# The first two filler weights go through value buffers instead of the stream's raw buffers

## The chip, the cores and the metric

The kernel runs on one core of a Trainium2 chip. The metric is device time in microseconds (us) of one execution, the median of several. A core has a matrix engine (PE), a vector engine (DVE), a scalar engine (ACT), a general engine (POOL) and a sync engine (SP) that here only issues DMAs. Each works through its own instructions in the order in which the program lists them; they wait for each other by semaphores. An instruction that waits holds up everything listed behind it on its engine.

## The reference

One layer over 1024 latent tokens of width 1024 with 256 context tokens. A modulated RMS norm is projected by one wide matrix `w_in` into the inputs of two branches, a gated linear attention (GLA) and a differential attention, and into two merge gates:

```
pl = project(modulate(x, sh_x, sc_x), w_in[layer])
o_gla = bidir_gla(q, k, v, la_f, la_b, s_f, s_b)
a = softmax(s1) - lam * softmax(s2);  o = a @ v          # per head, per block of queries
...
y = sigmoid(m_gla) * (a @ w_br_gla) + sigmoid(m_diff) * (b @ w_br_diff)
return y @ w_out
```

All in float32 (`x + g_x * out_x` at the end). `m_gla` and `m_diff` are 2048 of the columns of `w_in`.

## The kernel before, in words

A float32 product is made of three fast matmuls: each operand is rounded by ACT to a short format (`hi`) and DVE takes the rest (`lo = raw - hi`); then hi*hi, hi*lo and lo*hi are summed in one bank of PSUM. So each weight tile costs one DMA, one ACT pass and one DVE pass before PE can use it.

The program is written by generators (tasks) that a small planner in the same file interleaves: it keeps an estimate of each engine's time, and always runs the due task with the lowest priority number. The order of instructions on every engine is fixed when the program is built. A wait that the planner did not foresee is therefore a wait in the middle of a fixed queue.

The stages that matter here:

- The stream of projections (`mm`, `ma` are its PSUM banks, `w` its rounded weights). Its last weights, 128 columns wide, come through `raw`, three buffers of 4 KB a partition. Beside it the GLA branch ends; its last transposes write `gpl` and `d_aT`.
- `to_gla` then opens the pools of the next stage: `wt` (four buffers for rounded filler weights, `hi` and `lo` of two weights), `ft` (two), `aq` (four, rotated queries), `vv` (three, values of the attention: `hi` and `lo` of one head and one ahead), `mb` (one bank of PSUM), and sets the event `ev_b2`.
- The attention: 64 units of a head and 128 queries. A unit has 12 score matmuls into PSUM (`s<-kk,aq`), three maxima on DVE, two exponentials on ACT (`e<-s`), a combination on DVE, ten 128x128 transposes on PE (`b<-ident,e`), rounding by ACT and POOL (`ac`, `at`). For each pair of units 30 matmuls with the values follow (`b<-at,vv`). The first exponential needs the banks and the memory of the stream (`p` among them), so it comes after the last stream results are stored (`d_m<-p`).
- The filler (`fill`): the remaining merge gate columns, then `w_br_gla`, then `w_br_diff`, 23 weight tiles of 1024x128. Each serves two half tiles of 24 matmuls with 512 columns (`mb<-h,wt`). They have the lowest priority on PE and go where the planner sees PE free. Four half tiles share two weights (weight 0, weight 1, weight 0, weight 1). `mb` is one bank: ACT must copy a half tile out (`ft<-mb`) before the next begins. From the fourth half tile on, `pace` holds half tile i back until unit int(1.3 i) has its scores.

In `fill`, `load` takes a `raw` buffer per weight and issues its DMA, beginning when the stream has taken its last one (`ev_w2`); `conv` rounds it into `wt` after `ev_b2`. What is not used up as filler follows the attention on `mc` banks (line 353 is every product, 379 every transpose, 211 every ACT, DVE and POOL instruction, 318 every DMA).

Of the kernel before, what the change touches and what calls it, by code (L numbers as in the profile page):

```python
# [9 lines left out]
F32 = mybir.dt.float32  # L10
F32R = mybir.dt.float32r
BF16 = mybir.dt.bfloat16
AF = mybir.ActivationFunctionType
ALU = mybir.AluOpType
# [5 lines left out]
P = 128  # L20
# [4 lines left out]
NK = D // P  # L25
# [220 lines left out]
class Hybrid:  # L246
# [16 lines left out]
        wt=("sbW", 4), ft=("sbW", 2), aq=("sbB2", 4), vv=("sbB2", 3),  # L263
# [1917 lines left out]
    def fill(self):  # L2181


        d, a = self.d, self.a
        todo = [(0, s, self.win, C_MG + s * P) for s in range(self.fill_from, 16)] + \
               [(1, s, a["w_br_gla"][0], s * P) for s in range(8)] + \
               [(2, s, a["w_br_diff"][0], s * P) for s in self.DT]
        evs = [[Event()] for _ in todo]
        ws = {}

        def load():
            for n, (kind, _, src, o) in enumerate(todo):
                yield from self.acq("raw")
                raw = self.t("raw", [P, NK, P])
                yield self.dma(raw, src[:, o:o + P].rearrange("(k p) c -> p k c", p=P))
                d.spawn(conv(n, raw), 0.0, prio=3)
            d.set(self.ev_loaded)

        def conv(n, raw):
            yield self.ev_b2  # L2200
            yield from self.acq("wt", 2)
            hi = self.t("wt", [P, NK, P], F32R)
            lo = self.t("wt", [P, NK, P], F32R)
            yield d.on("ACT", raw)
            self.act.activation(hi, raw, AF.Copy)
            yield d.on("DVE", hi)
            e = self.dve.tensor_tensor(lo, raw, hi.bitcast(F32), ALU.subtract)
            self.rel("raw", e)
            ws[n] = (hi, lo)
            d.set(evs[n][0], e)  # L2210

        yield self.ev_w2
        d.spawn(load(), prio=3)
        yield self.ev_b2

        def bank():
            return "mc" if "psC" in self.pools else self.FI
# [14 lines left out]
        def half_tile(n, half, rhs):  # L2232
            kind, s, _, _ = todo[n]
            yield evs[n][0]
            hi, lo = ws[n]
            tg = bank()
            yield from self.acq(tg)
            pm = self.t(tg, [P, 512])
            mt = None
            if kind == 1:  # L2240
                yield from self.acq("ft")
                mt = self.t("ft", [P, 512])
                self.dma(mt, self.d_m[0][s][:, half * 512:(half + 1) * 512])
            elif kind == 2:
                d.spawn(self.load_y(s, half), prio=-1)
            for k in range(NK):
                if kind:
                    yield rhs.ev[k, half]
                e = self.mm3(pm, hi[:, k], lo[:, k], rhs[0][k][half], rhs[1][k][half], k == 0, k == NK - 1)
                yield AtPE(0)  # L2250
            if half == 1:
                self.rel("wt", e, 2)
            if kind == 2:
                d.spawn(self.post_y(tg, s, half, pm), e, prio=-1)
            else:
                d.spawn(post(tg, kind, s, half, pm, mt), e, prio=self.PP)
            return e
# [38 lines left out]
        n = 0  # L2296
        while n < len(todo):
# [8 lines left out]
            for half in range(2):  # L2306
                for x in two:
                    if i >= 3:
                        yield pace(i)
                    e = yield from half_tile(x, half, rhs)  # L2310
# [327 lines left out]
```

## Time and profile before

| what | value |
|---|---|
| runs | 1713.74, 1712.67, 1710.38 us, median 1712.67 |
| profiled execution | 1711.51 us, of which 1709.8 us are the span of the instructions |
| mean granted PE clock | 0.986 |
| PE busy | 1647.3 us, 96% of the span |
| DVE, ACT, POOL busy | 1208.6, 818.1, 638.2 us (71, 48, 37%) |
| start of the filler and of the scores | 983.4 us, 996.7 us |
| end of the filler on `mb` | 1511 us |

The profile comes from one execution. Busy is time in an instruction; a matmul counts as busy while it streams. The time in brackets behind a row of the timeline is how long the engine had been idle before it, with what released it. "PEclk" is the share of the full clock that PE was granted.

### The profile page before, as it was taken

The page shows a single profiled execution, that of the slowest core. Times are in us where ns is not written, and L with a number is a line of the kernel's source. Part 1 is how long each engine was busy: PE and PEld are TensorE (multiplying, and loading weights), DVE is VectorE, ACT ScalarE, POOL GpSimd, SP SyncE. Part 2 cuts the span into 40 slices and gives each one's busy share as a digit, 9 for nine tenths or more (in the row PEclk, how much of TensorE's full clock was granted, in tenths as well). Part 3 has the DMA queues.
Part 4 walks back from the last instruction along what each step waited for, and adds up shares of the span by engine and source line. Part 5 has one row for each costly group of instructions (what it writes and reads, how often), then busy time and mean ns, then how long its engine had stood idle before and what let it go on. Part 6 is the DMA issues. An engine that isn't in the chain of part 4 may idle for free.

```text
span 1709.8 us, 24608 instructions
## 1 busy us (share of the span) xinstructions
PE 1647.3 (96%) x8381; PEld 1364.0 (80%) x8381; DVE 1208.6 (71%) x1948; ACT 818.1 (48%) x1633; POOL 638.2 (37%) x651
## 2 busy tenths in 40 slices
PE   8899999999999999999999989999999999999999
PEld 3687887888788878788888768888878888887887
DVE  4773976875935465767776659887887888747694
ACT  4784555454432344343333346666665566542231
POOL 1600552552300012334454524555755566640000
PEclk9999999999999999999999999999999999999999
DMA  8537545653334474458899663543594534157421
GB/s 306 196 134 241 167 146 173 194 163 124 99 111 154 154 248 140 141 180 268 268 307 309 183 167 100 135 114 99 154 300 126 141 111 128 59 167 264 148 99 74
DMA packets 262974, 290.29 MB, mean 170 GB/s; under 512 B 23192, under 2 KB 185920, under 8 KB 262848
## 3 DMA queue, kind: packets, MB, share of 16 engines
q1 hardware_dynamic: 262848, 288.71, 54.1%
q8 instruction: 66, 1.08, 0.3%
q14 instruction: 60, 0.49, 0.1%
HBM read 192.70 MB, written 95.94 MB: 169 GB/s over the span
## 4 chain that ended last, share of the span: by engine, by line
PE 68%; DVE 14%; ACT 6%; POOL 5%; issue 4%; DMA 3%; SPq 0%; ACTq 0%; DVEq 0%; POOLq 0%
PE mm L353 15%; PE mc L353 9%; PE ma L353 8%; PE s L353 6%; PE mb L353 5%; PE gs L353 5%; DVE sm L211 4%; PE b L353 4%; PE go L353 4%; PE gt L353 3%; PE b L379 3%; ACT e L211 3%; PE tp L353 2%; DVE e L211 2%; POOL sm L211 2%
## 5 line engine op out<-in xcount | busy, mean ns | idle before, releaser
L353 PE MATMUL mm<-w,h 128*128 128x512 f32 x864 | 215.4, 398 | 2.8 <-DVE gb L211 2.0
L211 DVE TENSOR_REDUCE sm<-s 128x1 f32<-128x1024 f32 (+1 forms) x192 | 197.2, 1038 | 27.3 <-PE s L353 25.5
L211 ACT ACTIVATE e<-s,sm 128x1280 f32<-128x1280 f32 x128 | 170.0, 1331 | 91.7 <-DVE sm L211 84.6
L353 PEld LDWEIGHTS mm<-w,h 128*128 128x128 f32 x864 | 159.5, 188 | 37.3 <-DVE gb L211 2.7
L211 POOL TENSOR_TENSOR at<-ac,at 128x512 fp32r<-128x512 f32 x128 | 184.2, 1439 | 10.7
L353 PE MATMUL s<-kk,aq 128*128 128x512 f32 (+1 forms) x768 | 178.3, 368 | 10.0 <-ACT e L211 9.7
L353 PE MATMUL mb<-h,wt 128*128 128x512 f32 x624 | 173.8, 409 | 10.1 <-ACT ft L211 6.2
L211 POOL TENSOR_SCALAR at<-ac 128x512 fp32r<-128x512 f32 x128 | 101.0, 789 | 204.2 <-ACT ac L211 183.2
L353 PE MATMUL mm<-h,w 128*128 128x512 f32 x624 | 156.9, 402 | 3.2 <-DVE w L211 2.1
L353 PEld LDWEIGHTS s<-kk,aq 128*128 128x128 f32 x768 | 124.1, 193 | 32.4 <-ACT e L211 16.0
L353 PEld LDWEIGHTS mm<-h,w 128*128 128x128 f32 x624 | 117.8, 193 | 30.0 <-DVE w L211 3.8
L353 PEld LDWEIGHTS mb<-h,wt 128*128 128x128 f32 x624 | 110.6, 190 | 30.5 <-ACT ft L211 6.9
L211 DVE TENSOR_TENSOR w<-raw,w 128x512 fp32r<-128x512 f32 (+1 forms) x117 | 88.7, 787 | 60.1 <-ACT w L211 59.9
L353 PE MATMUL b<-at,vv 128*128 128x256 f32 x960 | 128.7, 282 | 1.6 <-ACT ac L211 0.8
L353 PEld LDWEIGHTS b<-at,vv 128*128 128x128 f32 x960 | 120.8, 188 | 6.5 <-POOL at L211 1.6
L353 PE MATMUL mc<-h,wt 128*128 128x512 f32 x480 | 113.1, 396 | 1.6 <-DVE wt L211 1.6
L211 POOL TENSOR_TENSOR sm<-sm,nhalf 128x8 f32<-128x8 f32 (+3 forms) x78 | 103.2, 1324 | 27.5 <-DVE sm L211 22.3
L211 DVE SCALAR_TENSOR_TENSOR e<-e,sm,e 128x1280 f32<-128x1280 f32 x64 | 112.4, 1756 | 1.3
L353 PEld LDWEIGHTS mc<-h,wt 128*128 128x128 f32 x480 | 90.9, 190 | 22.2 <-DVE wt L211 2.5
L211 ACT ACTIVATE ac<-b 128x512 f32<-128x512 f32 x121 | 72.0, 599 | 63.2 <-PE b L379 62.5
L353 PE MATMUL ma<-w,h 128*128 128x512 f32 x384 | 96.6, 396 | 0.4 <-DVE gp L211 0.4
L379 PE MATMUL b<-ident,e 128*128 128x128 f32 x604 | 88.8, 277 | 3.3 <-DVE at L211 1.5
(378 smaller groups left out, 3163.0 us busy)
## 6 DMA issues: line engine op xcount, KB each, us to landing
raw<-in_w_in SPq DMA_DIRECT2D x39, 512.0 KB, 4.4
rb<-in_w_in SPq DMA_DIRECT2D x64, 256.0 KB, 2.9
aq<-d_qT SPq DMA_DIRECT2D x128, 128.0 KB, 3.5
d_kT<-pl SPq DMA_DIRECT2D x40, 256.0 KB, 2.4
d_dv<-pl SPq DMA_DIRECT2D x40, 256.0 KB, 2.1
kk<-d_kT SPq DMA_DIRECT2D x32, 320.0 KB, 4.9
gv<-d_v SPq DMA_DIRECT2D x40, 256.0 KB, 4.5
vv<-d_dv SPq DMA_DIRECT2D x16, 640.0 KB, 6.3
```

The costliest lines, as they stand in the source:

```text
L211: self.ins = f(out, *args, **kw).ins
L353: self.ins = self.nc.tensor.matmul(out, lhsT, rhs, start=start, stop=stop, skip_group_check=more).ins
L379: self.nc.tensor.transpose(out, src, self.ident[:n, :n])
```

## The change

Weights 0 and 1 of the filler leave `load` and `conv`. When `ev_b2` comes, `fill` takes all four `wt` buffers and two of the three `vv` buffers, issues both DMAs into the `vv` buffers (eight of their ten 128-column blocks), and spawns `first` for each, with priority -1 instead of 3: the same ACT pass and the same DVE pass, after which the `vv` buffer is free again. `load` now begins at `ev_b2` too, and with weight 2.

```diff
         def load():
             for n, (kind, _, src, o) in enumerate(todo):
+                if n < 2:
+                    continue
                 yield from self.acq("raw")
                 raw = self.t("raw", [P, NK, P])
                 yield self.dma(raw, src[:, o:o + P].rearrange("(k p) c -> p k c", p=P))
@@ after conv @@
+        def first(n, raw):
+            hi, lo = ws[n] = tuple(self.t("wt", [P, NK, P], F32R) for _ in range(2))
+            yield d.on("ACT", raw)
+            self.act.activation(hi, raw, AF.Copy)
+            yield d.on("DVE", hi)
+            e = self.dve.tensor_tensor(lo, raw, hi.bitcast(F32), ALU.subtract)
+            self.rel("vv", e)
+            d.set(evs[n][0], e)
+
-        yield self.ev_w2
+        yield self.ev_b2
+        yield from self.acq("wt", 4)
+        yield from self.acq("vv", 2)
+        for n in range(2):
+            _, _, src, o = todo[n]
+            raw = self.t("vv", [P, 10, P])[:, :NK]
+            self.dma(raw, src[:, o:o + P].rearrange("(k p) c -> p k c", p=P))
+            d.spawn(first(n, raw), d.when(raw), prio=-1)
         d.spawn(load(), prio=3)
-        yield self.ev_b2
```

Since the planner's times shift, the order moves on all engines from here on. With the running numbers of the buffers left out, the orders of the two kernels are the same again on PE from about unit 38 of the attention to the end. Three places:

SP at the stage's begin, before: `aq` are the queries of units 2 and 3, `d_dv` the stored values, `d_kT` the keys, `in_w_in` the weights; `raw_9410` is weight 1 (weight 0 stands ahead of the `aq` rows, in `raw_9345`).

```order
L318 DMA aq_9342<-d_qT_86 64x2x256 x2
L318 DMA d_qT_87<-pl_9373 128x4x128
L318 DMA d_qT_87<-pl_9374 128x4x128
L318 DMA vv_9391<-d_dv_82 128x10x128
L318 DMA vv_9393<-d_dv_84 128x10x128
L318 DMA vv_9395<-d_dv_82 128x10x128
L318 DMA kk_9404<-d_kT_88 64x1280
L318 DMA kk_9404<-d_kT_90 64x1280
L318 DMA raw_9410<-in_w_in 128x8x128
L318 DMA d_qT_87<-pl_9426 128x4x128
```

And now, where `raw_9349` with weight 2 stands ahead of the `aq` rows:

```order
L318 DMA aq_9342<-d_qT_86 64x2x256 x2
L318 DMA vv_9345<-in_w_in 128x8x128
L318 DMA vv_9347<-in_w_in 128x8x128
L318 DMA d_qT_87<-pl_9377 128x4x128
L318 DMA d_qT_87<-pl_9378 128x4x128
L318 DMA vv_9395<-d_dv_82 128x10x128
L318 DMA kk_9404<-d_kT_88 64x1280
L318 DMA kk_9404<-d_kT_90 64x1280
L318 DMA d_qT_87<-pl_9427 128x4x128
L318 DMA d_qT_87<-pl_9428 128x4x128
L318 DMA vv_9441<-d_dv_84 128x10x128
L318 DMA raw_9443<-in_w_in 128x8x128
```

Weight 1 moved ahead of three values and two keys, weight 0 behind the queries, and of the first three values two moved back.

ACT at the same place, before; `ft_9478` copies the first half tile out of `mb`, the two `p` are the stream's last results:

```order
L211 ACTIVATE wt_9412<-raw_9345 128x1024
L211 ACTIVATE pl_9426<-tp_9421 128x512
L211 ACTIVATE p_9442<-mm_9305 128x512
L211 ACTIVATE p_9445<-mm_9306 128x512
L211 ACTIVATE wt_9475<-raw_9410 128x1024
L211 ACTIVATE ft_9478<-mb_9448 128x512
L211 ACTIVATE e_1993_9514,sm_9495<-s_1988_9494,sm_9497 128x1280
```

And now:

```order
L211 ACTIVATE wt_9410<-vv_9345 128x1024
L211 ACTIVATE pl_9427<-tp_9420 128x512
L211 ACTIVATE wt_9425<-vv_9347 128x1024
L211 ACTIVATE p_9460<-mm_9305 128x512
L211 ACTIVATE p_9463<-mm_9306 128x512
L211 ACTIVATE ft_9481<-mb_9445 128x512
L211 ACTIVATE ft_9511<-mb_9484 128x512
L211 ACTIVATE e_1997_9546,sm_9527<-s_1992_9526,sm_9529 128x1280
```

The rounding of weight 1 no longer stands directly ahead of the copy of the first half tile, and a second half tile is copied out ahead of the first exponential.

PE in units 2 and 3, before; the rows of `mb_9629` are the third half tile, which goes on behind the last row:

```order
L353 MATMUL s_1988_9494<-kk_7465,aq_9339 128x512 x4
L379 MATMUL b_2011_9592<-ident,e_1993_9514 128x128 x4
L353 MATMUL s_1988_9494<-kk_7465,aq_9339 128x256 x2
L353 MATMUL s_1988_9494<-kk_7468,aq_9342 128x256 x2
L353 MATMUL s_1988_9494<-kk_7468,aq_9342 128x512 x4
L379 MATMUL b_2020_9622<-ident,e_1993_9514 128x128 x4
L353 MATMUL mb_9629<-h_169_701,wt_9412 128x512
L353 MATMUL mb_9629<-h_170_702,wt_9412 128x512
L353 MATMUL mb_9629<-h_169_701,wt_9413 128x512
L353 MATMUL mb_9629<-h_172_704,wt_9412 128x512
```

And now, where the third half tile (`mb_9514`) is already through:

```order
L353 MATMUL s_1992_9526<-kk_7465,aq_9339 128x512 x4
L379 MATMUL b_2015_9623<-ident,e_1997_9546 128x128 x4
L353 MATMUL s_1992_9526<-kk_7465,aq_9339 128x256 x2
L353 MATMUL s_1992_9526<-kk_7468,aq_9342 128x256 x2
L353 MATMUL s_1992_9526<-kk_7468,aq_9342 128x512 x4
L379 MATMUL b_2024_9653<-ident,e_1997_9546 128x128 x4
L379 MATMUL b_2028_9666<-ident,e_2003_9588 128x128 x4
L353 MATMUL s_1992_9526<-kk_7465,aq_9339 128x512 x4
L379 MATMUL b_2030_9678<-ident,e_2003_9588 128x128 x4
L353 MATMUL s_1992_9526<-kk_7465,aq_9339 128x256 x2
```

Between the scores of units 2 and 3 no filler is left; only transposes stand there. Counted over the whole rows, the filler matmuls behind the scores of units 0 to 3 were 12, 9, 9 and 15 and are 12, 9, 0 and 9; ahead of unit 0 stood 27 and now stand 51.

## The prediction

> **What bounds the kernel now.** I read the page first, then the chain of work that ended last, then the timeline and windows around the stage's begin. The page:
>
> ```profile
> span 1709.8 us, 24608 instructions
> PE 1647.3 (96%) x8381; PEld 1364.0 (80%) x8381; DVE 1208.6 (71%) x1948; ACT 818.1 (48%) x1633; POOL 638.2 (37%) x651
> PE 68%; DVE 14%; ACT 6%; POOL 5%; issue 4%; DMA 3%; SPq 0%; ACTq 0%; DVEq 0%; POOLq 0%
> ```
>
> PE is busy 96% of the span and holds 68% of the chain. The change neither adds nor removes a matmul, so the time moves by what PE idles and by what it loses to a lower clock. One piece of the chain stands where the change is (start us, us, what), and two others give the prices of matmuls:
>
> ```profile
> 985.20 8.46 DMA raw<-in_w_in
> 1129.94 2.12 PE b L353 x18
> 1541.15 99.51 PE mc L353 x427
> ```
>
> A 512-column product costs 99.51/427 = 0.233 us, a 256-column one 2.12/18 = 0.118; so 12 scores (8 and 4 of them) cost 2.3 us. The timeline there:
>
> ```profile
> 969.82 1.71 SPq L318 DMA_DIRECT2D raw<-in_w_in  x2
> 971.58 5.11 SPq L318 DMA_DIRECT2D aq<-d_qT  x8
> 975.63 1.05 ACT L211 ACTIVATE wt<-raw 128x1024 fp32r<-128x1024 f32 x1
> 976.79 1.09 SPq L318 DMA_DIRECT2D d_qT<-pl  x2
> 981.24 2.32 PE L353 MATMUL mm<-h,w 128*128 128x512 f32 x9
> 982.76 1.22 DVE L211 TENSOR_TENSOR wt<-raw,wt 128x1024 fp32r<-128x1024 f32 x1
> 983.40 5.96 PE L353 MATMUL mb<-h,wt 128*128 128x512 f32 x24
> 985.20 0.58 SPq L318 DMA_DIRECT2D raw<-in_w_in  x1
> 988.10 4.29 SPq L318 DMA_DIRECT2D d_m<-p  x2
> 993.67 1.06 ACT L211 ACTIVATE wt<-raw 128x1024 fp32r<-128x1024 f32 x1 [9.48 <-DMA raw<-in_w_in]
> 994.64 0.58 ACT L211 ACTIVATE ft<-mb 128x512 f32<-128x512 f32 x1
> 995.27 1.65 PE L353 MATMUL mb<-h,wt 128*128 128x512 f32 x3 [5.91 <-ACT ft L211]
> 996.72 3.57 PE L353 MATMUL s<-kk,aq 128*128 128x512 f32 x12
> 1000.92 1.33 ACT L211 ACTIVATE e<-s,sm 128x1280 f32<-128x1280 f32 x1 [5.71 <-DVE sm L211]
> ```
>
> PE ends the first half tile at 989.36 and needs the bank `mb` emptied. The copy (`ft`, 0.58 us) stands on ACT behind the rounding of weight 1, whose DMA was issued only at 985.20, behind values and keys. So a DMA wait on ACT became 5.91 us of idle PE. What followed (length, then busy time of PE, PEld, DVE, ACT, POOL, then PEclk, DMA share, GB/s):
>
> ```profile
> 989.40:995.20 5.80, 0.00 (x0) 0.00 (x0) 0.44 (x1) 1.52 (x2) 0.00 (x0) 0.75 1.13 284
> 995.20:999.00 3.80, 3.73 (x10) 2.97 (x11) 1.13 (x2) 0.02 (x1) 0.00 (x0) 0.50 1.08 334
> 1050.20:1052.90 2.70, 0.07 (x2) 0.04 (x1) 2.63 (x6) 1.51 (x3) 1.03 (x1) 1.00 0.19 64
> 1053.90:1057.10 3.20, 3.20 (x13) 2.75 (x12) 3.13 (x5) 2.34 (x5) 3.12 (x3) 0.50 0.45 108
> 1093.90:1097.00 3.10, 3.10 (x19) 2.73 (x20) 3.00 (x4) 1.98 (x4) 2.04 (x2) 1.00 0.25 86
> 996.00:1021.60 25.60, 24.88 (x120) 19.87 (x118) 20.36 (x29) 12.40 (x20) 8.10 (x8) 0.94 0.43 124
> 1021.60:1141.30 119.70, 114.31 (x704) 99.31 (x705) 104.83 (x152) 77.32 (x145) 64.93 (x60) 0.99 0.41 109
> ```
>
> After the gap the clock is 0.50 for 3.8 us (1.9 us of work lost). After a stall of 2.63 us at 1050.2 it is 0.50 for 3.2 us (1.6 us); after one of 1.57 us ahead of 1093.9 it stays at 1.00.
>
> **The change part by part.** The counts of DMAs, roundings and matmuls stay; only places move.
>
> *First weights.* SP issues both behind the last `aq`, at 976.7, where `d_qT<-pl` stands now. Landing:
>
> ```profile
> raw<-in_w_in SPq DMA_DIRECT2D x39, 512.0 KB, 4.4
> raw<-in_w_in SPq DMA_DIRECT2D x5, 512.0 KB, 5.6
> kk<-d_kT SPq DMA_DIRECT2D x2, 320.0 KB, 7.7
> ```
>
> The first row is the whole kernel, the others 965 to 1000 us. With little queued ahead I take 5.0: weight 0 lands at 981.7, weight 1 some 2 us later (512 KB at 284 GB/s take 1.8). Ends: 4.4, and the 8.46 of the chain. ACT (1.06) ends at 982.8, DVE (1.22) at 984.1. PE has six of the nine `mm` matmuls to do, until 982.6, begins with `hi` at 982.9 and waits again for `lo`: about 1.0 us idle. The rest of the half tile and three `mm` matmuls, 25 x 0.233 = 5.8, end at 989.9; before it was 989.36.
>
> *The copy.* ACT has rounded weight 1 by then (lands about 983.7, ready by 985.0 on ACT, 986.3 on DVE). So the gap is the copy and its handover, 0.58 + 0.1 = 0.7 us; this removes 5.2 us of idle and the 1.9 of clock. Half tile two runs from 990.6 to 996.2, a second 0.7 us copy follows, three matmuls, and unit 0 has its scores at 997.6, not 996.72, but at full clock: its first four end at 998.5 (before: DVE took them up at 998.66 in the row below). DVE and ACT therefore begin the attention at the same time, and PE is 24 matmuls, 5.6 us, ahead.
>
> ```profile
> 998.66 1.82 DVE L211 TENSOR_REDUCE sm<-s 128x1 f32<-128x1024 f32 x2 [2.67 <-PE s L353]
> 1007.70 1.19 PE L353 MATMUL s<-kk,aq 128*128 128x512 f32 x4 [0.30 <-ACT e L211]
> 1011.36 2.41 DVE L211 SCALAR_TENSOR_TENSOR e<-e,sm,e 128x1280 f32<-128x1280 f32 x1
> 1013.47 1.08 PE L353 MATMUL s<-kk,aq 128*128 128x512 f32 x4
> 1020.14 1.33 ACT L211 ACTIVATE e<-s,sm 128x1280 f32<-128x1280 f32 x1 [2.50 <-DVE sm L211]
> 1021.61 1.20 PE L353 MATMUL s<-kk,aq 128*128 128x512 f32 x4 [0.25 <-ACT e L211]
> ```
>
> *Units 0 to 3 give most of it back.* Units 2 to 4 begin at 1007.70, 1013.47 and 1021.61, and PE waits for exponentials there, which wait for DVE: the chain DVE to ACT sets the pace, not PE. The new order has no filler behind unit 2's scores and nine matmuls, not 15, behind unit 3's, so PE idles where it had worked. Unit 4 starts at the same 1021.6. By then PE has done 9 filler matmuls (81 against 72) and 6 value matmuls more, 4 transposes less (0.1 each): 2.1 + 0.7 - 0.4 = 2.4 us is what is left of the 5.6.
>
> *Units 4 to 19.* Half tile 8 starts behind unit 19 in both orders, so by 1141.3 (start of unit 20 before) both have the same work done. Before, these 119.7 us hold 5.4 us of idle and 1.7 of lower clock (1.6, and 0.1 around it): 112.6 of work. Now 112.6 - 2.4 = 110.2 remain, plus stalls. The long stall before, 2.63 us, fell in unit 8, where only four transposes stood between two sets of scores. In the new order the thinnest units of this stretch have 5.5 us of PE work (units 11 and 14), the others 6 to 9.6, against the 5.5 to 5.8 between starts of units in the rows above where DVE paced them. So I take the small stalls of before (5.4 - 2.63 - 1.57 = 1.2) and two of 1.5: 4.2 us, ends 1.2 and 9. DVE would then be busy 104.8 of 114.4 us, 92%. Units 4 to 19 take 114.4 for 119.7: a gain of 5.3.
>
> *Costs.* The third weight's rounding on DVE (1.22) moves into unit 3, ahead of the small maximum that releases an exponential; half of it, 0.6 us, is charged, ends 0 and 1.2. Values: `lo` of head 0 waits for a `vv` buffer, free at 984.1; the first value matmul ran at 1024.5, so some 35 us cover it. The store `d_m<-p`, which the first exponential also waits for, has 1.0 MB more ahead of it, 3.7 us at 284 GB/s:
>
> ```profile
> DMA to landing us min/median/max: 7.5/7.5/7.5
> ```
>
> From 988.1 it landed at 995.6, now about 999.3, against 1000.9 when it is needed: nothing, with 1.6 us to spare; beyond that each microsecond delays every unit. After unit 38 the order is the same; nothing there.
>
> **Sum** against the profiled execution, 1711.51 us (span 1709.8): 5.3 - 0.6 = 4.7 less, 1706.8. It stands 1.2 below the median of the runs, 1712.67; I add half of that: 1707.4, 0.3% under the median. About 0.2%, 3.4 us, is what a measurement tells from no change.
>
> **The rivals.**
> - *The clock falls in units 2 and 3.* PE stalls there for about 0.4, 2.3 (transposes that need DVE's combination of 1011.36 + 2.41) and 0.9 us within 8. The row at 1093.9 (1.57, no fall) speaks against it, that at 1053.9 (2.63, fall) for it. Price 1.6: 1709.0. [...]
> - *DVE keeps its pace.* If DVE stays at 104.8/119.7 = 88% busy, as its gaps come from its own chain with ACT, the stretch takes 119.7 again: 1711.5 + 0.6, with the same offset 1712.7.
> - *Late landing.* At 8.46 us weight 0 lands at 985.2; unit 0 and all units come 3.5 us later: 1710.9, or more if that gap lowers the clock.
> - *All of it is kept.* With stalls of 1.2 instead of 4.2: 1704.4.
> - *Slower: long stalls.* The denser units 4 to 19 leave DVE no slack, and a late maximum stalls PE for 2.63 us with a fall of the clock, 4.2 together, like unit 8 before. With four of them the loss is 16.8 where 4.2 were counted: 1720. From three on (12.6, 1715.8) it is slower than before by the bound.
>
> **How the numbers follow.** Forecast 0.40, clock 0.20, DVE's pace 0.15, late 0.07, all kept 0.10, slower 0.08. Faster by over 0.2% (under 1709.2): nearly all of the forecast (0.36), half of the clock's case, all of the last gain: 0.56. Slower takes 0.08 and 0.03 of the pace and late cases; same is the rest, 0.33. The range 1702.5 to 1713.0 leaves out the slower case and the tails of the others, 0.16. The forecast's own is 1704.4 to 1709.2.
>
> **What would show it.** In the changed kernel's trace: PE's wait of 5.9 us for `ft` gone, two of 0.7 in its place, granted clock 1.00 until unit 2 (right), or a wait of over 2 us for `wt` (late landing); unit 0's scores near 997.6 and unit 4's near 1021.6; idle of 4 to 5 us in units 2 and 3; unit 20 near 1136 instead of 1141.3; from unit 38 on a constant lead. Wrong I am if unit 4 comes well before or after 1021.6, if PE's waits for `e` in units 4 to 19 exceed 9 us, or if a lead at unit 38 is lost by the end.

## The result, and the profile after

The changed kernel took 1697.86 us (median of 4, 1696.93 to 1698.88) where the kernel before took 1711.53 (1709.70 to 1713.74): a ratio of 0.9928 with an interval of 0.9915 to 0.9940. Forecast were 1707.4 us, in a range of 1702.5 to 1713.0. Faster was right, the size was not: 4.7 us less than the profiled execution were forecast. Further executions of both kernels were timed beside the experiments. Over all of them the changed kernel holds 1699.0 us on average (15 executions, 1696.9 to 1701.9) and the kernel before 1711.1 (78, 1704.4 to 1716.7). So the change is worth about 12 us, and it is those 12 that have to be explained.

The page after:

```profile
span 1695.4 us, 24607 instructions
PE 1635.8 (96%) x8381; PEld 1354.9 (80%) x8381; DVE 1203.3 (71%) x1948; ACT 818.6 (48%) x1633; POOL 636.3 (38%) x651
```

The span fell by 14.4 us and PE's busy time by 11.5 (1647.3 before), with the same 8381 matmuls. A matmul counts as busy while it streams: in the profile of before, three products of 512 columns took 1.65 us from 995.27 us, at a granted clock of 0.50, and 0.85 from 1003.78, at 1.00. So most of the gain is the same work at a higher clock, not less idle time. The timeline where the change is:

```profile
975.69 1.22 SPq L318 DMA_DIRECT2D vv<-in_w_in  x2
981.54 1.06 ACT L211 ACTIVATE wt<-vv 128x1024 fp32r<-128x1024 f32 x1 [6.84 <-DMA vv<-in_w_in]
982.65 0.73 PE L353 MATMUL mb<-h,wt 128*128 128x512 f32 x2 [0.81 <-ACT wt L211]
983.91 1.21 PE L353 MATMUL mb<-h,wt 128*128 128x512 f32 x4 [0.53 <-DVE wt L211]
989.99 0.60 ACT L211 ACTIVATE ft<-mb 128x512 f32<-128x512 f32 x1 [3.52 <-PE mb L353]
990.64 5.78 PE L353 MATMUL mb<-h,wt 128*128 128x512 f32 x24 [0.69 <-ACT ft L211]
997.10 0.97 PE L353 MATMUL mb<-h,wt 128*128 128x512 f32 x3 [0.69 <-ACT ft L211]
997.90 2.45 PE L353 MATMUL s<-kk,aq 128*128 128x512 f32 x12
1013.50 0.63 PE L379 MATMUL b<-ident,e 128*128 128x128 f32 x4 [1.62 <-DVE e L211]
1016.24 1.68 PE L353 MATMUL s<-kk,aq 128*128 128x256 f32 x8 [0.75 <-ACT e L211]
1020.97 1.08 PE L353 MATMUL s<-kk,aq 128*128 128x512 f32 x4
```

The gap of 5.91 us became two waits of 0.69; 0.81 and 0.53 us of waiting for weight 0 are new; units 2 and 3 have waits of 1.62 and 0.75. Now four stretches: from 960 us to the start of unit 4, to unit 20, to unit 38, and to the last product (length, busy time of PE, PEld, DVE, ACT, POOL, then PEclk, DMA share, GB/s). Before:

```profile
960.00:1021.61 61.61, 54.56 (x252) 42.91 (x251) 36.48 (x55) 24.26 (x46) 21.69 (x22) 0.94 0.66 177
1021.61:1141.32 119.71, 114.33 (x704) 99.33 (x705) 104.85 (x152) 77.33 (x145) 64.94 (x60) 0.99 0.41 109
1141.32:1283.30 141.98, 136.06 (x849) 117.24 (x848) 118.60 (x174) 89.00 (x178) 86.28 (x77) 1.00 0.63 183
1283.30:1705.94 422.64, 413.19 (x2242) 351.42 (x2240) 309.07 (x470) 188.91 (x357) 146.54 (x130) 0.98 0.43 132
```

And after:

```profile
960.00:1020.97 60.97, 54.74 (x258) 42.79 (x257) 35.44 (x55) 26.58 (x48) 21.52 (x21) 1.00 0.65 184
1020.97:1133.97 113.00, 110.28 (x701) 96.41 (x700) 101.45 (x151) 75.42 (x144) 66.36 (x62) 1.00 0.42 111
1133.97:1274.03 140.06, 134.40 (x844) 116.99 (x842) 116.03 (x174) 89.09 (x177) 83.83 (x75) 1.00 0.64 186
1274.03:1691.54 417.51, 407.58 (x2242) 346.94 (x2240) 309.54 (x470) 188.74 (x357) 147.11 (x130) 1.00 0.44 134
```

Length less PE's busy time is PE's idle time. In the last stretch both kernels run the same instructions in the same order, idle time is 9.45 and 9.93 us, and yet it is 5.1 us shorter: the clock is 1.00 instead of 0.98. My prediction had put nothing there.

In these two profiles the granted clock goes down to 0.50 for 3.41 or 6.83 us at a time, one or two periods, and in each profile the starts lie on one grid (before, the first is at 26.27 us and the last within the work at 1541.79: 1515.52 us, 444 times 3.4133). With the lowered periods listed, each stretch splits into idle time and work lost to the clock (half of PE's busy time in its lowered periods, as they run at 0.50; with PE busy for all of 3.41 us that is 1.7). A lowered period counts for the stretch of the wait ahead of it; the one at 1282 us, behind a wait in unit 37, counts for units 20 to 37. The lengths themselves can't be subtracted, because ahead of unit 38 the two kernels do different work in a stretch. The means of three profiles of each kernel, in us:

| stretch | forecast gain | idle before, after | lost to the clock before, after | gain in both together |
|---|---|---|---|---|
| 960 us to unit 4 | 2.4 | 7.6, 5.8 | 2.4, 0 | 4.2 |
| units 4 to 19 | 2.9 less 0.6 | 5.5, 2.7 | 0.6, 0 | 3.3 |
| units 20 to 37 | 0 | 5.9, 5.7 | 0.6, 0 | 0.7 |
| unit 38 to the end | 0 | 9.4, 9.8 | 4.3, 1.0 | 3.0 |

The sum is 11.3, of the 12.1 between the means of all executions. 4.5 of it is idle time, 6.8 the clock. The timed executions agree: their mean granted clock is 0.9880 before (74 that list it) and 0.9919 after (15), and 0.0039 of some 1705 us is 6.7 us.

### The profile page after: what moved, and what is told of

Read it like the earlier page. It is cut to its first block, busy times and chain, and to the rows that moved or that the text cites. A ratio compares the mean times of both kernels' runs of the same rounds, so it can differ in the third digit from the quotient of the medians.

```text
span 1695.4 us, 24607 instructions
## 1 busy us (share of the span) xinstructions
PE 1635.8 (96%) x8381; PEld 1354.9 (80%) x8381; DVE 1203.3 (71%) x1948; ACT 818.6 (48%) x1633; POOL 636.3 (38%) x651
## 4 chain that ended last, share of the span: by engine, by line
PE 68%; DVE 14%; ACT 5%; POOL 4%; issue 4%; DMA 3%; SPq 1%; ACTq 0%; DVEq 0%; POOLq 0%
PE mm L353 16%; PE mc L353 9%; PE ma L353 8%; PE s L353 6%; PE mb L353 5%; PE gs L353 5%; PE b L353 4%; DVE sm L211 4%; PE go L353 3%; PE gt L353 3%; PE b L379 3%; PE tp L353 2%; DVE e L211 2%; ACT e L211 2%; POOL sm L211 2%
## 5 line engine op out<-in xcount | busy, mean ns | idle before, releaser
L353 PE MATMUL s<-kk,aq 128*128 128x512 f32 (+1 forms) x768 | 174.0, 360 | 6.9 <-ACT e L211 6.9
L211 POOL TENSOR_SCALAR at<-ac 128x512 fp32r<-128x512 f32 x128 | 96.9, 757 | 188.8 <-ACT ac L211 184.7
```

The lines of the kernel that those rows point to most:

```text
L211: self.ins = f(out, *args, **kw).ins
L353: self.ins = self.nc.tensor.matmul(out, lhsT, rhs, start=start, stop=stop, skip_group_check=more).ins
```

## The experiments

**Both kernels again.** The same programs in other executions, to see what of the two profiles repeats.

> The kernel before, unchanged, in other executions. In the two profiles the granted clock is 0.5 in whole periods of 3.41 us (or two of them), always the period behind one in which PE was idle for about half of it; the grid of these periods lies 1.7 us apart in the two executions. Theory A (chance of the grid): where the grid lies against PE's waits differs in each execution, so this profile lowers the clock at other waits than the first did. Laying the grid at 60 places over the first profile, with under 0.54 busy as the condition, gives 3 to 7 lowered periods after 960 us (mean 5.1; the profile had 7), 1.7 us each. Mean clock then 0.985 to 0.990 and times 1706 to 1713 us. Theory B (place): the same waits lower the clock again in every execution: the same 7 periods, 0.986, 1711 to 1712 us, and lowered periods again near 1282, 1347, 1473 and 1541 us.

> A third profile of the kernel before. The timed runs of the kernel before hold 1710.6 us on average with a spread of 1704 to 1717, the profiled ones 5.9 and 6.5 us of gap before unit 0. If the grid decides by chance, the lowered periods behind unit 38 (4 and 2 so far) are 1 to 3 here, at some of the same waits near 1344, 1471 and 1538 us; if the place decides, 4 again.

> The changed kernel, unchanged, in other executions. Theory A (chance of the grid): the profile shown had no lowered period from 960 us to the end of the work; the grid laid over it at 60 places gives 1 to 4 (mean 2.4), so this profile has one to three of them, at the waits near 1334, 1460 or 1525 us, mean clock 0.990 to 0.992, times 1698 to 1702 us; against the kernel before 7.8 us less on average (3.2 of idle, 2.7 periods of 1.7). Theory B (place): again none from 960 us on, 0.993, 1697 us, 14 us less.

> The changed kernel once more, beside the two others. Ten runs of it so far hold 1698.9 us on average (1696.9 to 1701.9), so 1698 to 1700 us; 11 to 13 us less than the kernel before; no lowered period between unit 0 and unit 38, none or one behind it.

Measured: the kernel before 1710.89 us (12 executions) and 1713.07 (one); the changed one 1699.56 (6), ratio 0.9940 (0.9922 to 0.9959), and 1699.51 (5), ratio 0.9930 (0.9916 to 0.9944). Behind unit 38 the profiles of before have three, two and three lowered periods, those of the changed kernel none, none and two. Here is one of the waits there, PE's for the bank `mb`, in two profiles of before (the first and the third):

```profile
1346.24 2.11 PE L353 MATMUL mb<-h,wt 128*128 128x512 f32 x6 [1.70 <-DVE ft L211]
```

```profile
1348.00 2.23 PE L353 MATMUL mb<-h,wt 128*128 128x512 f32 x6 [1.80 <-DVE ft L211]
```

and the period of 3.41 us in which it lies, with the next one, in the same two profiles:

```profile
1343.81:1347.22 3.41, 1.63 (x8) 1.26 (x9) 3.38 (x7) 2.77 (x5) 2.31 (x3) 1.00 0.93 195
1347.22:1350.64 3.42, 3.42 (x11) 2.67 (x11) 2.35 (x3) 0.00 (x0) 3.34 (x3) 0.50 0.50 160
```

```profile
1345.42:1348.83 3.41, 1.50 (x9) 1.12 (x9) 3.38 (x7) 2.82 (x5) 2.27 (x3) 1.00 0.88 185
1348.83:1352.24 3.41, 3.41 (x11) 2.66 (x10) 2.21 (x3) 0.00 (x0) 3.33 (x3) 0.50 0.58 182
```

The same wait in the first and the second profile of the changed kernel, with its periods:

```profile
1335.90 1.66 PE L353 MATMUL mb<-h,wt 128*128 128x512 f32 x6 [1.76 <-DVE ft L211]
```

```profile
1331.91:1335.32 3.41, 2.10 (x13) 1.30 (x11) 3.34 (x7) 3.41 (x11) 2.20 (x3) 1.00 1.16 269
1335.32:1338.73 3.41, 2.83 (x14) 2.35 (x15) 2.50 (x5) 0.85 (x3) 2.51 (x3) 1.00 0.35 109
```

```profile
1335.27:1338.68 3.41, 1.96 (x12) 1.23 (x10) 3.34 (x7) 3.41 (x12) 2.23 (x3) 1.00 1.17 263
1338.68:1342.09 3.41, 2.96 (x16) 2.49 (x17) 2.50 (x5) 0.69 (x3) 2.51 (x3) 1.00 0.38 120
```

The wait is equally long. Before, it begins 0.7 us into its period (1346.24 - 1.70 = 1344.54, against 1343.81; 0.8 in the other two profiles), fills half of it, and the next period runs at 0.50. In the changed kernel it begins 2.2 us into the period (2.1 and 1.8 in the other two), is split between two, neither under 0.50 busy, and the clock stays. The margin is thin in the third profile: 1.57 us of the wait lie in one period, which is 0.50 busy, where 0.44 to 0.48 lowered the clock before. Theory A had the places within the periods differ by chance from one execution to the next; at the first wait, near 47 us, they do (0.9, 0.6 and 2.2 us into its period before; 1.9, 0.2 and 1.4 after), but late in the program they repeat within 0.1 us before and 0.4 after. So theory B was nearer: a kernel has its own lowered periods. Why the places draw together is not shown; my guess is that each lowered period, by delaying the program by up to 1.7 us, moves the next waits on.

**The gap remade.** The copy of the first half tile done ten times, on ACT alone, with the planner not told.

```diff
+                if s == todo[0][1] and half == 0:
+                    for _ in range(9):
+                        self.act.eng.activation(mt, pm, AF.Tanh, scale=0.5)
                 self.rel(tg, self.act.activation(mt, pm, AF.Tanh, scale=0.5))
```

> The changed kernel, with the copy of the first half tile done ten times instead of once, 9 x 0.6 = 5.4 us more on ACT with the order of all engines kept: PE gets the gap of 6 us back that the change took away. Theory 1 (as predicted: units 2 and 3 give most of a lead back): unit 0 is 5.4 us later, PE's idle time of 3.1 us in units 0 to 3 goes, DVE and ACT begin the units late too, so unit 4 comes 5 us later, and with the clock lowered behind the gap (1.7 to 3.4 us) the whole is 5 to 8 us slower than the changed kernel. Theory 2 (the gap was covered): units 2 and 3 take it up and the end moves by under 2 us.

Measured: 1706.91 us, against 1699.56 for the changed kernel beside it: 7.4 slower. Against the kernel before the ratio is 0.9978 (0.9966 to 0.9990). The wait and the first two stretches:

```profile
997.02 7.97 PE L353 MATMUL mb<-h,wt 128*128 128x512 f32 x24 [6.34 <-ACT ft L211]
```

```profile
960.00:1029.49 69.49, 57.90 (x262) 45.20 (x261) 35.44 (x56) 32.02 (x57) 22.37 (x22) 0.95 0.57 161
1029.49:1142.45 112.96, 110.30 (x701) 96.35 (x699) 101.47 (x151) 75.47 (x144) 66.33 (x62) 1.00 0.41 112
```

The gap and its lowered clock (idle 11.6 us in the first stretch, where the changed kernel has 5.8; 2.4 lost to the clock) arrive at the end in full. Units 4 to 19 are as in the changed kernel to 0.04 us. That is theory 1's number, but not its mechanism: the idle time of units 0 to 3 did not go (3.0 us, 3.1 in the changed kernel). So the gap is worth 7.4 of the 12.

The other 4 to 5 are not simply what the new order of the units gains. Against the three profiles of before, this kernel has 4.0 us more of idle time and lost clock up to unit 4 (14.0 for 10.0), then 3.4 less in units 4 to 19, 0.8 less to unit 38, and 3.7 less behind it, where its one profile has no lowered period (over its 12 executions the mean granted clock is 0.9905, against 0.9881 for the kernel before beside them, which is 4 us):

```profile
1282.56:1699.83 417.27, 407.23 (x2242) 346.80 (x2240) 309.47 (x470) 188.79 (x357) 147.36 (x130) 1.00 0.43 134
```

What the new order costs ahead of unit 4 and saves in units 4 to 19 nearly cancels; what is left is mostly the clock in the part with the unchanged order.

**Weight 1 alone.** Against the kernel before: `load` skips only weight 1, which goes through `vv` with the function `first` of the change; weight 0 stays in `raw`, ahead of the queries.

```diff
+                if n == 1:
+                    continue
...
         yield self.ev_b2
+        yield from self.acq("wt", 2)
+        yield from self.acq("vv")
+        _, _, src, o = todo[1]
+        raw = self.t("vv", [P, 10, P])[:, :NK]
+        self.dma(raw, src[:, o:o + P].rearrange("(k p) c -> p k c", p=P))
+        d.spawn(first(1, raw), d.when(raw), prio=-1)
```

> Only weight 1 goes through a value buffer; weight 0 keeps its raw buffer and its DMA ahead of the queries. Its order is that of the kernel before again from unit 19 on. Theory 1 (weight 1 alone carries the change): the copy of the first half tile finds ACT free, the gap of 5.9 us shrinks to 0.7, and PE has no wait of 0.8 and 0.5 us for weight 0 as the changed kernel has: 0 to 2 us faster than the changed kernel up to unit 20, within 3 us of it at the end. Theory 2 (both are needed): the third weight's rounding or weight 1's landing behind the queries makes a new wait of over 2 us before unit 0, and the time stays within 4 us of the kernel before.

Measured: 1701.54 us (ratio 0.9950, 0.9931 to 0.9969), 2.0 over the changed kernel beside it. At the end that is theory 1: moving weight 1 alone brings some 9 of the 12 us. Up to unit 20 it is not ahead (1135.18 us; the changed kernel has 1133.97 to 1137.27). The first two stretches:

```profile
960.00:1015.00 55.00, 53.55 (x252) 42.65 (x251) 34.20 (x55) 23.96 (x45) 17.30 (x18) 1.00 0.75 199
1015.00:1135.18 120.18, 115.02 (x704) 99.82 (x703) 103.05 (x153) 77.82 (x146) 69.44 (x63) 0.97 0.40 108
```

Unit 4 starts 6 us sooner, with 1.5 us of idle time. Then units 4 to 19 give it back: 5.2 us idle and two lowered periods (3.4), behind waits of 2.1 and 2.3 us in units that hold 3.0 and 5.2 us of PE work.

**Smoother orders for weight 1 alone.** First the planner's `SLACK` at 1.1 for the whole program, then 1.1 until unit 20 only, and 1.2 until unit 10.

```diff
+        def slack():
+            d.SLACK = 1.1
+            yield self.ev_u[20]
+            d.SLACK = Driver.SLACK
+        d.spawn(slack(), prio=-9)
```

> Weight 1 alone through a value buffer, and the planner's lookahead SLACK at 1.1 instead of 1.0, which shifts the order everywhere; it is chosen because no unit behind unit 1 then holds less than 4.8 us of PE work (unit 8 held 2.7 in the kernel before and with weight 1 alone, and the clock fell there). Theory 1 (thin units make the waits, and weight 0 is better loaded early): PE's waits at units 8 and 13 go with their two lowered periods, so 5 to 7 us under the 1701.5 us of weight 1 alone, 1695 us, under the changed kernel. Theory 2 (DVE sets the pace there): the waits move to other units, 1699 to 1703 us.

> Weight 1 alone through a value buffer, and the planner's SLACK at 1.1 from the filler's begin until unit 20 only; from unit 38 on the order is that of both kernels, and before the filler it is unchanged. The thinnest unit of 2 to 19 holds 4.8 us of PE work (2.7 with weight 1 alone). Theory 1 (thin units make the waits): PE's idle time from unit 4 to 20 falls from 5.2 us (weight 1 alone) to 2 to 3 and the lowered periods at 1048 and 1082 (3.4 us) go: 5 to 6 us under weight 1 alone, 1695 to 1697 us, 2 to 4 us under the changed kernel. Theory 2 (DVE sets the pace): the idle time stays near 5 us and moves to other units: 1700 to 1702 us, no better than the changed kernel.

> The same with SLACK 1.2 until unit 10 only: another order, thinnest units 9 (4.9 us) and 18 (4.8), and 40 and 56 as in both kernels. Theory 1: as the kernel with 1.1 until unit 20, 1695 to 1697 us. Theory 2: 1700 to 1702 us.

Measured: 1703.98, 1698.74 and 1700.24 us; the changed kernel beside the last two 1699.51. With 1.1 until unit 20, units 4 to 19 and the last stretch:

```profile
1017.27:1129.11 111.84, 108.47 (x683) 93.34 (x681) 101.04 (x151) 73.60 (x141) 65.97 (x61) 1.00 0.40 107
1274.12:1696.71 422.59, 412.86 (x2242) 351.06 (x2240) 309.31 (x470) 188.76 (x357) 146.38 (x130) 0.99 0.43 133
```

Units 4 to 19 do nearly as theory 1 said: 3.4 us of idle time in both (2 to 3 forecast, 5 by theory 2), no lowered period. So thin units made the long waits of this stretch, not DVE's pace. The times didn't follow. Units 32 to 37 have 3.6 us of idle time (weight 1 alone 3.2, the changed kernel 2.0), and from its end on the clock was lowered at 1273, 1338, 1464 and 1533 us (with 1.2: the first three), where weight 1 alone had one lowered period. The wait ahead of the second starts 0.75 and 0.2 us into its period; in the kernel before it was 0.7. With `SLACK` 1.1 throughout, 4.2 us more idle time before 960 us and 6.4 more in units 38 to 49 outweighed the rest. None of the three is shown to beat the changed kernel.

**The place in the period, moved.** Repeats of one matmul in unit 41: busy PE, same result, same order. Seven in the changed kernel, nine in the kernel before (the line that sets `self.extra` at first is left out).

```diff
+                if k == 0 and self.ev_u[38].t is not None and not self.extra:
+                    self.extra = True
+                    for _ in range(7):
+                        self.nc.tensor.matmul(pm, hi[:, k], rhs[0][k][half], start=True, stop=True)
```

> The changed kernel with one matmul of the filler half tile in unit 41 done seven times more (same result): 7 x 0.233 = 1.6 us of busy PE, no idle, order kept. The profiles showed that where PE's late waits stand in the periods of 3.41 us repeats: in three executions of the changed kernel the wait at 1334 to 1337 us begins 2.0 to 2.2 us into its period, so that no period holds half of its 1.76 us, and in three of the kernel before 0.7 to 0.8 us into it, all within one period, and the clock fell each time. Theory D (place in the period): 1.6 us later this wait lies 0.3 us into a period, the clock is lowered behind it, and the kernel is 1.6 + 1.7 = 3.3 us slower than the changed one: 1702 us, a lowered period near 1338. Theory B' (the place in the program alone decides): 1.6 us slower at most, no lowered period there.

> The kernel before with nine such extra matmuls in unit 41, 2.1 us of busy PE. Theory D: the wait at 1344 to 1346 moves from 0.75 to 2.85 us into its period and is split 0.56 to 1.2; the clock isn't lowered, so the wait at 1471 comes 2.1 - 1.7 = 0.4 later in its period, at 1.6 instead of 1.2, and is split too. The lowered periods at 1347 and 1473 (in all three profiles) go, 1.7 + 1.5 us: the kernel does 2.1 us of useless work more and is 1 to 3 us faster than the kernel before, 1708 to 1710 us. Theory B': the lowered periods stay, 2.1 us slower.

Measured: 1699.64 us for the changed kernel with 1.6 us of work more, where 1702 was expected. As stated, theory B' came nearer: no lowered period at 1338 and less than 1.6 us of cost. The wait at 1335 began 3.3 us into its period, so that 1.56 of its 1.69 us lie in the next one. That period is 0.54 busy, and the clock stayed; the period of the next long wait was 0.43 busy, and there the clock fell to 0.50, as it did in one of the three profiles of the changed kernel:

```profile
1335.25:1338.66 3.41, 1.85 (x8) 1.54 (x9) 3.27 (x6) 1.90 (x4) 2.43 (x3) 1.00 0.76 192
1338.66:1342.07 3.41, 3.41 (x22) 2.71 (x20) 2.61 (x3) 2.20 (x3) 3.33 (x4) 1.00 0.64 192
1461.54:1464.96 3.42, 1.45 (x8) 1.22 (x9) 3.19 (x8) 1.91 (x3) 1.74 (x3) 1.00 0.05 20
1464.96:1468.37 3.41, 3.41 (x12) 2.88 (x11) 1.90 (x4) 2.51 (x4) 2.47 (x3) 0.50 0.46 145
```

So this run does not show theory D: the place missed what was meant, and with 1.56 us of the wait in one period the clock stayed at 1.00. The kernel before with 2.1 us more: 1712.73 us, ratio 1.0002 (0.9993 to 1.0011), so 0.3 us, between -1.2 and 1.9; the 2.1 of theory B' lies outside. The profile is as theory D has it: the waits begin 2.6 and 2.0 us into their periods, and no period behind unit 41 is lowered:

```profile
1347.36:1350.77 3.41, 2.45 (x15) 1.60 (x13) 3.34 (x6) 3.18 (x11) 2.13 (x3) 1.00 1.16 283
1350.77:1354.18 3.41, 2.56 (x12) 2.09 (x13) 2.60 (x5) 1.19 (x3) 2.51 (x2) 1.00 0.51 145
1473.65:1477.06 3.41, 1.98 (x14) 1.52 (x12) 3.38 (x5) 1.26 (x9) 3.33 (x3) 1.00 0.39 116
1477.06:1480.47 3.41, 2.06 (x13) 1.83 (x14) 3.21 (x6) 2.17 (x4) 1.73 (x3) 1.00 0.20 77
```

The timed executions agree: a mean granted clock of 0.9891 against 0.9875 for the kernel before beside them, which is 2.7 us. The 2.1 us of useless work cost 0.3, with the two waits split between periods that were 0.58 to 0.75 busy; that it makes the kernel faster, as theory D said, is not shown.

**Waits put into PE's stream.** POOL rewrites part of a weight (same values) between two products that read it, in half tiles behind the attention. The edit of the kernel with groups of three; the other three differ in the half tiles, in `k` and in the number of rewrites, and the lines that count `self.halves` are left out:

```diff
+                if tg == "mc" and self.halves in (2, 4, 6, 8, 10, 12) and k in (3,):
+                    for _ in range(3):
+                        self.pool.eng.tensor_scalar(hi[:, k:k + 2], hi.bitcast(F32)[:, k:k + 2], 1.0, None, ALU.mult)
```

> The changed kernel with waits put into PE's stream behind the attention, where PE is otherwise busy: in six half tiles of the filler on the mc banks, POOL rewrites two blocks of the rounded weight (same values) between two products that read them, three times in a row (about 0.4 us each), at two places 2.8 us of work apart. So PE gets twelve waits of about 1.5 us. Theory A (the clock falls behind a period of 3.41 us with PE idle for about half): none or one of the waits fills half a period, the clock stays, and the cost is the idle time alone, about 12 x 1.5 = 18 us. Theory C (the clock follows the share of idle time over longer stretches, or each wait costs its own fall): the same cost as the kernel with six long waits, over 25 us.

> As the kernel with twelve short waits, but with the same 36 rewrites in groups of six: six waits of about 2.8 us, the same idle time or 1 to 3 us less (six handovers fewer). Theory A: a wait of 2.8 us leaves a period of 3.41 us under half busy at about 0.8 of the places where the grid can lie, so 4 to 6 lowered periods of 1.7 us each: 7 to 10 us of lower clock, and the kernel is 4 to 9 us slower than the one with short waits though PE idles no longer. Theory C: no slower than the one with short waits, 0 to 3 us faster.

Measured: 1752.12 and 1753.40 us. This pair was mis-sized: a rewrite took 0.9 us (three 2.71 at 1523.49 us), not 0.4, so the short waits were 2.4 to 3.3 us and the long ones 5.4 to 6.8. Both lowered the clock (a mean of 0.982 and 0.977 in the two profiles, 0.993 in the changed kernel's), and the pair tells the theories apart no further. Hence the second pair, 18 rewrites singly or in threes:

> Waits put into PE's stream behind the attention again, with sizes that the first two such kernels showed (0.9 us for each rewrite on POOL): in nine half tiles of the changed kernel one rewrite at two places 2.8 us of work apart, 18 waits of about 0.9 us, 16 us of idle. Theory A (clock falls behind a period with PE idle for about half): no lowered period behind 1515 us, the cost is 16 us, about 1715 us. Theory C (idle time over longer stretches decides): lowered periods as many as with six waits of 2.7.

> The same 18 rewrites in six groups of three: six waits of 2.7 us, 16 us of idle. Theory A: four to six lowered periods of 1.7 us, 7 to 10 us slower than the kernel with 18 short waits, about 1724 us. Theory C: the same time as that kernel.

Measured: 1721.07 us (1718.63 to 1722.32) and 1730.64 (1728.96 to 1734.14), 9.6 us apart. The time alone does not decide, because the groups also waited longer; the clock does. The products there and the stretch with most of the waits, singly:

```profile
L353 PE MATMUL mc<-h,wt 128*128 128x512 f32 x427 | 105.2, 401 | 17.2 <-POOL wt L2269 15.6 <-DVE wt L211 1.6
1535.00:1660.00 125.00, 113.00 (x476) 88.47 (x476) 82.96 (x124) 26.34 (x40) 12.79 (x14) 1.00 0.47 152
```

and in threes:

```profile
L353 PE MATMUL mc<-h,wt 128*128 128x512 f32 x450 | 115.2, 419 | 22.4 <-POOL wt L2269 20.7 <-DVE wt L211 1.6
1535.00:1660.00 125.00, 106.53 (x417) 84.73 (x418) 72.95 (x108) 21.79 (x32) 17.54 (x15) 0.90 0.49 157
```

Behind the 18 waits of 0.75 to 1.3 us, 15.6 us in all, nothing was lowered (1.00 from 1535 to 1660 us). With the six of 2.6 to 4.0 us the clock there was 0.90 on average: seven lowered periods with 10 us of work lost in them (one, 1.7, behind a wait for `wt` that the other kernel has as well). That is theory A. The groups also waited 5.1 us longer than the single rewrites (20.7 for 15.6), and the two profiles lie further apart (spans 1717.2 and 1732.4) than the medians. Nor did every long wait lower the clock: one of the six, 3.40 us up to 1582.71, is split between two periods that are 0.52 and 0.48 busy, and neither is followed by a lowered one:

```profile
1577.53:1580.94 3.41, 1.78 (x8) 1.13 (x6) 3.34 (x6) 0.64 (x1) 1.62 (x2) 1.00 0.44 144
1580.94:1584.36 3.42, 1.65 (x7) 1.39 (x8) 1.78 (x3) 0.00 (x0) 1.64 (x2) 1.00 0.03 10
1584.36:1587.77 3.41, 3.41 (x17) 2.79 (x16) 1.96 (x3) 1.06 (x1) 0.00 (x0) 1.00 0.01 2
```

## Why the prediction was wrong

Of the 6.5 us between the forecast gain of 4.7 and the 11.2 of the table, 3.0 lie behind unit 38, 1.8 ahead of unit 4, 1.0 in units 4 to 19 and 0.7 in units 20 to 37.

- **The gap.** Right in kind: 5.91 us became 0.69, and its removal was put at 5.2 + 1.9 = 7.1; remade, it cost 7.4. It was sized on the one profile with the shortest gap: the other two have 6.5 and 7.1 us, and 2.6 us lost to the clock. About 1 us of the missing gain.
- **Weight 0's wait and the begin of unit 0** were nearly right: 1.3 us for 1.0, unit 0 at 997.9 for 997.6, unit 4 at 1020.97 for 1021.6.
- **"Units 0 to 3 give most of it back"** described the two orders, not the gap. The idle time in units 0 to 3 was 3.1 us (0.4 + 2.3 + 0.9 = 3.6 forecast, though the signs at the prediction's end say 4 to 5), but it is 3.0 with the gap remade as well. Nothing of the gap is given back; the new order, with 24 more matmuls ahead of unit 0, costs that time either way.
- **Units 4 to 19** have 2.7 us of idle time in all three profiles, where 4.2 was taken from ends of 1.2 and 9: neither of the two stalls of 1.5 came (the longest wait in the first profile is 0.77), and the small ones came to more than 1.2. DVE was busy 101.45/113.00 = 90%, 92 forecast and 88 before.
- **The third weight's rounding** was charged 0.6; no wait in the trace shows it.
- **"After unit 38 the order is the same; nothing there"** is the step that failed: a term put at nothing, with the order as its only reason. The lead was to stay constant from unit 38 on; in the two profiles it was 9.3 us there (1283.30 against 1274.03) and 14.4 at the last product. The idle time there is the same, and over three profiles of each kernel 3.0 us of the gain came from it, because waits of the same length lay otherwise in the clock's periods. I had seen the same kind of price twice (a stall of 2.63 us with a fall, one of 1.57 without) and used it only where the order changes.
- **The rivals.** The clock did not fall in units 2 and 3: in the changed kernel's profile the period with the wait of 1.62 us (1011.07 to 1014.49) was busy for 1.80 of its 3.42 us, transposes included, the next one ran at 1.00, and up to unit 4 the mean is 1.00 in all three profiles. How transposes count for the clock is not shown. In the changed kernel's profile the period from 24.62 to 28.03 us holds no PE work but transposes, 2.40 us of them, and the clock stayed at 1.00 behind it; in that of before the one from 22.86 to 26.27 holds 2.26 us of PE work, the last products and then transposes, and the next ran at 0.50. DVE's pace, a late landing and long stalls did not occur. "All of it is kept" was nearest, 1704.4, still 5 us too high.

## What to carry over

Sum idle time and lost clock apart, and look at the lowered periods along the whole program, not only where the order changes: here the late wait for `mb` began 0.7 us into its period before and 2.2 after, though the order there was the same. In the kernel before, its 1.70 us lay within one period, and the next one, 3.42 us of busy PE at 0.50, lost 1.7 more; the 18 waits of 0.75 to 1.3 us, 2.8 us of work apart, lowered nothing. Take the size of a stall from several profiles when a DMA's landing decides it.

## What the runs showed of the hardware

In the first profiles of the two kernels the granted clock is 0.50 in eight stretches of 3.41 us and six of 6.83, and once more at the end of each. From 20 us on, these are the periods at full clock with PE busy for up to 0.71 of them (start in us, busy share), by whether the next one ran at 0.50:

| profile | next at 0.50 | next at 1.00 |
|---|---|---|
| before | 1705.63 0.09, 268.62 0.12, 425.63 0.15, 988.83 0.16, 1050.27 0.24, 46.75 0.26, 1470.11 0.36, 1278.97 0.42, 1343.82 0.48, 1538.38 0.52, 22.86 0.66 | 698.70 0.44, 1091.23 0.54, 1408.67 0.55, 125.26 0.67 |
| after | 423.98 0.15, 1690.32 0.36, 45.10 0.42, 270.38 0.46, 123.60 0.59 | 1458.22 0.50, 1011.07 0.53, 130.43 0.58, 697.04 0.60, 1331.92 0.61, 1270.48 0.64, 980.35 0.65, 1396.78 0.65, 1461.63 0.68, 24.62 0.70, 1144.19 0.70, 21.20 0.71 |

All other periods at full clock from 20 us on were busier, and the next ran at 1.00. So in these executions a period with PE idle for about half of it was followed by a lowered one in some cases (0.42, 0.46, 0.48 and 0.52 busy) and not in others (0.44, 0.50, 0.53, 0.54). What decides there is open, and so is why the places of the late waits repeat.

Three rewrites of 128x256 elements of a weight in place took POOL 2.71 us at 1523.49 and 3.41 at 1579.09 in the kernel with groups of three at two places, 0.90 and 1.14 each. Its rounding of 128x512 elements from one buffer into another took 0.79 us on average in the profile of before and 0.76 in that of the changed kernel (128 each).
